# Query, key, value and four gate tiles of a hybrid layer: seven block products ahead of the attentions instead of plain products between them

## The chip, the cores and the metric

One core of a Trainium2 chip. The time is the device time of one execution in microseconds (us); of several runs the median is given. TensorE (PE) multiplies, ScalarE (ACT) and VectorE (DVE) work on SBUF and PSUM, GpSimd (POOL) does small work and issues some transfers, and SyncE (SP) issues most of them. PEld is TensorE's loading of weights, which overlaps its matmuls.

## The reference

One layer of an encoder for two requests that share all weights: a prompt of 1024 tokens and a sample of 32 tokens with a cache of 512. Model width 1024, 8 heads of 64 in either attention, feed-forward width 2816.

```python
ada = silu(c) @ w_ada + b_ada            # sh1, sc1, gt1, sh2, sc2, gt2
h = rms_norm(x, g_pre_mix) * (1 + sc1) + sh1
p = h @ w_in    # q-latent 384 | kv-latent 256 | rope key 32 | sb q 512 | sb k 512 | sb v 512 | gate A 1024 | gate B 1024
o_a = block-causal latent attention (softmax)
# o_b, stick-breaking attention, strictly causal:
z = q @ k.T * SB_SCALE
sp = where(mask, softplus(z), 0)
later = reverse_cumsum(sp) - sp
a = where(mask, exp(log_sigmoid(z) - later), 0);  o_b = a @ v
merged = sigmoid(g_a) * (o_a @ w_proj_a) + sigmoid(g_b) * (o_b @ w_proj_b)
x = x + gt1 * rms_norm(merged @ w_out, g_post_mix)
x = x + gt2 * rms_norm(conv_ffn(rms_norm(x, g_pre_ffn) * (1 + sc2) + sh2), g_post_ffn)
```

Outputs are both requests' rows, the latents, rope keys, keys and values of both, and the last rows of the convolution's state. All of it is float32.

## The kernel before

Both requests lie side by side as 1056 columns (1024 + 32): the activations are held transposed, 8 tiles of 128 features by 1056 tokens. Every float32 product is three matmuls: each operand is split into a high part (rounded by ACT, `hi`, L65) and a low part (the rest, subtracted by DVE, `lo`, L68), and `mm3` (L72 to L74) multiplies high by high, low by high and high by low into one PSUM bank.

`stage_h` is the opening. It loads the rows of x, scales them (`load`), computes the modulation of the norm in two halves (`ada_half(0)` and `ada_half(1)`: eight weight tiles from DRAM, four small matmuls each at L252, a copy, two transposes at L257, and the gain at L236), and turns the rows by TensorE (`norm_T`, L281); ACT applies gain and shift (`hf`), DVE casts the high part (L290) and takes the low one (L291). The result is `Hh` and `Hl`. The second half of the features needs the second gain.

`stage_sb` then runs four pairs of heads. Each `sb_pair` first makes its query, key and value tile of 128 columns of `w_in` with `mtile`: three blocks of 352 columns by 8 k by 3, 72 matmuls a tile. Queries and keys are split into parts, keys and values are turned into natural rows for the outputs (`to_natural`, L400) and stored on POOL's queue (L446). Then the pair's two heads go through attention block by block. The order of its work is written out by hand as a string of tokens, `ORDER`: S is a score (L473 and L474), a and e the two sigmoids on ACT, c a scan and x a product on DVE, T a transpose (L591), h and v its two parts, V the values (L605), o and p the output. Between them stand the filler tokens: f is one step of a generator `gates`, which computes a gate tile of `w_in` (72 matmuls, four tiles in each pair) and a few weight products of the modulation (`ada_step`), G takes its result out, D sums the modulation, W and w split the next weights. TensorE, ACT, DVE and POOL each keep that order. After each second pair `sb_sample` does the sample's attention (L747 and near it). A pair's first score follows its own value tile at once, so a new pair begins with 216 matmuls of products. `stage_lat` and the latent attention, the merge and the feed-forward follow; the feed-forward's up-projection already multiplies in halves with seven products instead of eight (L1683 to L1685).

Of the kernel before, what the change touches and what calls it, by code (L numbers as in the profile page):

```python
# [41 lines left out]
PARTS = ((0, 0, 96), (96, 80, 16), (112, 64, 16))  # L42


class K:
# [107 lines left out]
    def late_vectors(self):  # L153

        nc, a = self.nc, self.a
        v = self.tl(self.At, [P, TP], F32, "A")
# [83 lines left out]
    def ada_half(self, hf, wp, tp):  # L240
# [4 lines left out]
        for k in range(KT):  # L245

            last = hf == 1 and k >= KT - 2
            w = self.tl(*((self.W, [P, 1024]) if last else (wp, [P, 2 * 512])), F32, "wr").rearrange("p (v n) -> p v n", v=2)
# [17 lines left out]
    def norm_T(self, t0, xs, g, sv, tp, k0=0, k1=KT):  # L266


        nc = self.nc
        if t0 < 8:  # L270
            n = len(xs) * P
            m = 512 // n
            c = slice(t0 * P, t0 * P + n)
            for k in range(k0, k1, m):
                tr = self.bank("tr")
                f = self.tl(tp, [P, 512], F32, "hf").rearrange("p (k c) -> p k c", k=m)
                for e in range(m):
                    kc = slice((k + e) * P, (k + e) * P + P)
                    for j, x in enumerate(xs):
                        o = e * n + j * P  # L280
                        nc.tensor.transpose(tr[:, o : o + P], x[:, kc], self.idt)  # L281
                h, l = self.Hht[:, k : k + m, c], self.Hlt[:, k : k + m, c]

                both = t0 == 4 and k0 == 0
                for e in range(m):
                    for x in (f, h) if both else (f,):
                        nc.scalar.activation(x[:, e], tr[:, e * n : e * n + n], AF.Identity,
                                             bias=self.adaT[:, sv, k + e, 0:1], scale=g[:, k + e, 0:1])
                if not both:
                    nc.vector.tensor_copy(h, f)  # L290
                nc.vector.tensor_tensor(l, f, h.bitcast(F32), ALU.subtract)  # L291
        else:
            tr = self.bank("tr")
            for c in range(2):
                nc.tensor.transpose(tr[:, c * P : c * P + P], xs[0][:, c * P : c * P + P], self.idt)
            f = self.tl(tp, [P, 512], F32, "hf")[:, :256].rearrange("p (k t) -> p k t", t=TS)
            for k in range(k0, k1):
                j, c = k // 2, k % 2
# [104 lines left out]
    def sb_pair(self, p):  # L403
# [33 lines left out]
        def ev_out(name, after=None):  # L437
            def ev(tr, t0, n, r):
# [8 lines left out]
                if after:  # L447
                    after(st, tr, t0, n, r)
# [1781 lines left out]
```

## Time and profile before

| what | us |
| --- | --- |
| median of 3 runs | 1736.81 (1736.24 to 1738.41) |
| the profiled execution | 1738.68 |
| its span | 1736.8 |
| PE busy | 1697.2 |
| DVE busy | 1206.2 |
| ACT busy | 909.9 |
| POOL busy | 279.3 |
| first score of pairs 0, 1, 2, 3 at | 84.83, 201.30, 323.74, 438.99 |
| last value product of pairs 0, 1, 3 at | 163.91, 279.17, 516.87 |

The span runs from the first to the last instruction; what lies around it in an execution is 1.9 us here. In rows of the timeline the first number is the start, the second the time to the end of the last of the xN instructions, and the bracket tells the engine's idle time before and what ended it. In rows of groups, busy time and the mean of one in ns follow the bar, then the idle time before.

### The profile page before, as it was taken

How to read it: one execution, taken by the hardware profiler on the slowest of the kernel's cores; microseconds unless marked ns; L12 is line 12 of the kernel's file. 1: busy time of each engine (PE TensorE's matmuls, PEld its weight loads, DVE VectorE, ACT ScalarE, POOL GpSimd, SP SyncE). 2: the span in 40 equal slices, each digit the busy share in tenths (PEclk: the TensorE clock that was granted, in tenths of full speed). 3: DMA queues.
4: the chain of work that ended last, by engine and by line, in shares of the span. 5: the costliest groups of instructions: out<-in, count | busy, mean ns of one | idle time of the engine just before them, and what ended most of it. 6: DMA issues, size and time to landing. Idle time of an engine off the chain costs nothing. (4 is left out here: it accounts for less than half of the span.)

```text
span 1736.8 us, 29763 instructions
## 1 busy us (share of the span) xinstructions
PE 1697.2 (98%) x11542; PEld 1548.3 (89%) x11542; DVE 1206.2 (69%) x1971; ACT 909.9 (52%) x1745; POOL 279.3 (16%) x586
## 2 busy tenths in 40 slices
PE   6999999999999999999999999999999999999998
PEld 3899999999999988989888779999999999977886
DVE  4576574574662587768785778877787787788456
ACT  5455453553552677767774277444454444544442
POOL 2211111211120011101100032221111121110013
PEclk8999999999999999999999999999999999999999
DMA  8243333333341222222245631434323323697753
GB/s 321 82 133 103 108 107 97 99 120 92 112 120 49 74 74 64 64 72 66 100 163 179 190 128 43 164 104 128 128 92 128 128 92 128 210 343 241 238 148 119
DMA packets 170094, 223.64 MB, mean 129 GB/s; under 512 B 12917, under 2 KB 117056, under 8 KB 169952
## 3 DMA queue, kind: packets, MB, share of 16 engines
q1 hardware_dynamic: 154336, 177.91, 32.3%
q0 software_dynamic: 15392, 43.74, 7.1%
q8 instruction: 91, 1.49, 0.4%
q14 instruction: 51, 0.42, 0.1%
q10 hardware_dynamic: 224, 0.09, 0.0%
HBM read 169.92 MB, written 51.25 MB: 127 GB/s over the span
## 5 line engine op out<-in xcount | busy, mean ns | idle before, releaser
L65 ACT ACTIVATE wh<-wr 128x1024 fp32r<-128x1024 f32 (+6 forms) x161 | 134.4, 846 | 261.6 <-PE s L1684 80.0
L68 DVE TENSOR_TENSOR wl<-wr,wh 128x1024 fp32r<-128x1024 f32 (+6 forms) x161 | 153.0, 959 | 140.9 <-ACT wh L65 140.5
L72 PE MATMUL mm<-hh,wh 128*128 128x352 f32 x696 | 234.7, 337 | 0.0
L73 PE MATMUL mm<-hl,wh 128*128 128x352 f32 x696 | 226.9, 326 | 0.3 <-DVE hl L291 0.2
L74 PE MATMUL mm<-hh,wl 128*128 128x352 f32 x696 | 227.2, 326 | 0.0
L72 PEld LDWEIGHTS mm<-hh,wh 128*128 128x128 f32 x696 | 131.8, 189 | 9.0 <-issue 5.4
L73 PEld LDWEIGHTS mm<-hl,wh 128*128 128x128 f32 x696 | 131.7, 189 | 3.9 <-DVE hl L291 1.7
L74 PEld LDWEIGHTS mm<-hh,wl 128*128 128x128 f32 x696 | 131.4, 189 | 1.7 <-issue 1.6
L68 DVE TENSOR_TENSOR PTl<-tr,PTh 128x512 fp32r<-128x512 f32 x100 | 68.3, 687 | 50.6 <-ACT PTh L65 50.2
L1685 PE MATMUL s<-T,wl 128*128 128x256 f32 (+1 forms) x328 | 93.6, 285 | 0.0
L1683 PE MATMUL s<-T,wh 128*128 128x256 f32 (+1 forms) x328 | 93.3, 284 | 0.0
L1684 PE MATMUL s<-T,wh 128*128 128x256 f32 (+1 forms) x328 | 93.2, 284 | 0.0
L1824 DVE SCALAR_TENSOR_TENSOR u<-u,c,u 128x1058 f32<-128x1058 f32 x68 | 87.1, 1318 | 2.0 <-ACT u L1821 0.7
L65 ACT ACTIVATE PTh<-tr 128x512 fp32r<-128x512 f32 x100 | 59.3, 597 | 53.8 <-PE tr L591 51.0
L591 PE MATMUL tr<-c,A 128*128 128x128 f32 x576 | 83.5, 274 | 0.6 <-DVE A L693 0.5
L1683 PE MATMUL tr<-T,wh 128*128 128x272 f32 (+1 forms) x272 | 77.9, 286 | 0.0
L1685 PE MATMUL tr<-T,wl 128*128 128x272 f32 (+1 forms) x272 | 77.6, 285 | 0.0
L1684 PE MATMUL tr<-T,wh 128*128 128x272 f32 (+1 forms) x272 | 77.5, 285 | 0.0
L68 DVE TENSOR_TENSOR wl<-S,wh 128x1024 fp32r<-128x1024 f32 x40 | 49.0, 1224 | 37.4 <-ACT wh L65 36.1
L591 PEld LDWEIGHTS tr<-c,A 128*128 128x128 f32 x576 | 68.1, 140 | 5.9 <-issue 1.6
L1685 PE MATMUL mm<-T,wl 128*128 128x256 f32 (+1 forms) x256 | 73.0, 286 | 0.3 <-DVE wl L68 0.2
L1683 PE MATMUL mm<-T,wh 128*128 128x256 f32 (+1 forms) x256 | 73.1, 286 | 0.0
(682 smaller groups left out, 5385.1 us busy)
## 6 DMA issues: line engine op xcount, KB each, us to landing
wr<-in_w_ada_dram SPq DMA_DIRECT2D x48, 512.0 KB, 4.6
wr<-in_w_up_dram SPq DMA_DIRECT2D x44, 512.0 KB, 4.2
dr<-in_w_down_dram SPq DMA_DIRECT2D x43, 512.0 KB, 6.0
wr<-in_w_in_dram SPq DMA_DIRECT2D x33, 512.0 KB, 4.4
wr<-gdn SPq DMA_DIRECT2D x30, 512.0 KB, 4.7
gdn<-u POOLq DMA_DIRECT2D x23, 512.0 KB, 5.0
gd<-nat POOLq DMA_DIRECT2D x48, 176.0 KB, 2.3
t<-gd SPq DMA_DIRECT2D x16, 528.0 KB, 5.1
```

The lines of the kernel that those rows point to most:

```text
L65: self.nc.scalar.activation(out, in_, AF.Identity, scale=scale)
L68: return self.nc.vector.tensor_tensor(out, full, hi.bitcast(F32), ALU.subtract)
L72: m(ps, lh, rh, start=start, stop=False)
L73: m(ps, lh, rl, start=False, stop=False)
L74: self.pe = m(ps, ll, rh, start=False, stop=stop).ins
L591: self.nc.tensor.transpose(tr[:, (2 * s + q) * P : (2 * s + q + 1) * P], at[q][:, b * P : b * P + P], self.idt)
L1683: m(ps[:, :n], w[0][:, k], x[0][:, k, c], start=first and k == 0, stop=False, skip_group_check=True)
L1684: m(ps[:, :n], w[0][:, k], x[1][:, k, c], start=False, stop=False, skip_group_check=True)
L1685: i = m(ps[:, :n], w[1][:, k], x[0][:, k, c], start=False, stop=k == 3, skip_group_check=True)
L1824: nc.vector.scalar_tensor_tensor(y, u[:, w : w + YW], self.cvT[:, w, cc : cc + 1], y, ALU.mult, ALU.add)
```

## The change

A tile pair's product is cut into halves: the pair's two tiles of 128 columns of `w_in` (A), the two halves of the 1024 features, and the two halves of the 1056 columns (HC = 528, as 256 and 272). Winograd's form needs seven products of half size: with B11 and B22 and so on the quarters of h, they go over B11, T1, B21, T2, T3, T4 and B22, where T1 = B12 - B11, T3 = B22 - B12, T2 = T3 + B11 and T4 = B21 - T2. The sums of h are made once, on DVE, with their high parts on ACT; the sums of weights are made for each pair of tiles. `z_prod` is one product of 24 matmuls, `z_out` takes it out (a copy on ACT, or an addition on DVE), and the steps a to g are the seven products of a group.

There are eight groups: two of gates (tiles 0 and 1, 2 and 3), and (q0,k0), (v0,v1), (q1,k1), (q2,k2), (v2,v3), (q3,k3). Steps a and b of the first two stand inside `stage_h`, ahead of `ada_half(1)`. A new `stage_in` does all the rest ahead of the attentions. `z_done` splits queries, keys and values and writes them to scratch in DRAM; `sb_load` brings them back for each pair on POOL's queue, for pair 0 right behind the last stores. The quarter B12 of h is parked in DRAM and split again by the filler token B inside pair 0. Twelve gate tiles are left as filler, three in a pair, in four blocks of 264 columns, as are the latents; the weight products of the modulation go 3, 3 and 2 with the three tiles of a pair; and `ORDER` is written anew for this. Cut to its core:

```diff
+        self.F = [[self.u_tile().rearrange("p (k c) -> p k c", k=2) for _ in range(2)] for _ in range(2)]
...
             for t in range(4):
                 load(t)
             self.ada_half(0, wp, tp)
             norm(0, 0)
-            w = [self.w_in_tile(672)]
+            g0, g1 = self.early = self.group(0), self.group(1)
+            self.raw_a(g0)
             for t in range(4, 8):
                 load(t)
...
+            self.raw_b(g0)
             norm(4, 0)
...
+            self.step_a(g0, "mm mm")
+            for i in range(2):
+                x = self.F[1][i]
+                self.plus(x, self.F[0][i], B11, i, ALU.subtract)
+                self.both(T1, x, i)
+            self.raw_a(g1)
+            self.step_b(g0, "mm mm")
+            self.raw_b(g1)
+            self.step_a(g1, "mm mm")
+            self.step_b(g1, "mm mm")
             self.ada_half(1, wp, tp)
-            nc.vector.tensor_scalar(xs, xs, self.rstd_s(xs, tp), None, ALU.mult)
             norm(0, 1)
-            norm(8, 0)
             norm(4, 1)
             norm(8, 1)
...
+    def plus(self, out, x, pair, i, op):
+        for b in pair:
+            self.nc.vector.tensor_tensor(out, x, b.bitcast(F32)[:, 2 * i : 2 * i + 2], op)
+            x = out
+    def both(self, d, x, i):
+        h, l = (y[:, 2 * i : 2 * i + 2] for y in d)
+        self.hi(h, x)
+        self.lo(l, x, h)
...
+    def unit(self, x):
+        if self.n_unit % 2 == 0:
+            self.wt = [self.tl(self.W, [P, 1024], F32R, t) for t in ("wh", "wl")]
+        i = 512 * (self.n_unit % 2)
+        self.n_unit += 1
+        h, l = (t[:, i : i + 512] for t in self.wt)
+        self.hi(h, x)
+        self.lo(l, x, h)
+        return [t.rearrange("p (k c) -> p k c", k=4) for t in (h, l)]
+    Z_BLK = ((0, 256), (256, 272))
+    def z_prod(self, w, x, tags=None, banks=None):
+        new = banks is None
+        if new:
+            banks = [self.bank(t) for t in tags.split()]
+        for (c0, n), ps in zip(self.Z_BLK, banks):
+            c = slice(c0, c0 + n)
+            for k in range(4):
+                for i, (p, q) in enumerate(((0, 0), (0, 1), (1, 0))):
+                    self.nc.tensor.matmul(ps[:, :n], w[p][:, k], x[q][:, k, c], start=new and k + i == 0,
+                                          stop=k == 3 and i == 2, skip_group_check=True)
+        return banks
+    def z_out(self, out, banks, x=None):
+        for (c0, n), ps in zip(self.Z_BLK, banks):
+            c = slice(c0, c0 + n)
+            if x is None:
+                self.nc.scalar.copy(out[:, c], ps[:, :n])
+            else:
+                self.nc.vector.tensor_tensor(out[:, c], ps[:, :n], x[:, c], ALU.add)
+    def step_a(self, g, tags):
+        w = self.unit(g["ra"][:, :512])
+        g["q1"] = self.tl(self.Zq, [P, HC], F32, "q1", 3)
+        self.z_out(g["q1"], self.z_prod(w, self.Z["B11"], tags))
+    def step_b(self, g, tags):
+        add = self.nc.vector.tensor_tensor
+        s = g["s1"] = self.tl(self.Zq, [P, 512], F32, "s1", 2)
+        add(s, g["rb"][:, :512], g["rb"][:, 512:], ALU.add)
+        w = self.unit(s)
+        q = g["q5"] = self.tl(self.Zq, [P, HC], F32, "q5", 2)
+        self.z_out(q, self.z_prod(w, self.Z["T1"], tags))
+        self.nc.gpsimd.tensor_tensor(q, q, g["q1"], ALU.add)
...
+    def step_d(self, g, tags):
+        ra, rb, add = g["ra"], g["rb"], self.nc.vector.tensor_tensor
+        add(rb[:, :512], ra[:, :512], rb[:, :512], ALU.subtract)
+        add(ra[:, :512], g["s1"], ra[:, :512], ALU.subtract)
+        X = g["X"] = self.z_prod(self.unit(ra[:, :512]), self.Z["T2"], tags)
+        g["q2"] = self.tl(self.Zp, [P, HC], F32, "q2", 2)
+        self.z_out(g["q2"], X, g["q5"])
+    def step_e(self, g):
+        self.z_prod(self.unit(g["rb"][:, :512]), self.Z["T3"], None, g["X"])
+        g["ub"] = self.u_tile()
+        self.z_out(g["ub"][:, HC:], g["X"], g["q5"])
+    def step_f(self, g):
+        self.z_prod(self.unit(g["rb"][:, 512:]), self.Z["T4"], None, g["X"])
+        self.z_out(g["ub"][:, :HC], g["X"], g["q1"])
+        self.z_done(g["cols"][1], g["ub"])
+    def step_g(self, g, tags):
+        ra = g["ra"]
+        self.nc.vector.tensor_tensor(ra[:, 512:], ra[:, 512:], ra[:, :512], ALU.subtract)
+        w = self.unit(ra[:, 512:])
+        self.z_out(g["ua"][:, HC:], self.z_prod(w, self.Z["B22"], tags), g["q2"])
+        self.z_done(g["cols"][0], g["ua"])
...
+        self.step_c(g0, "s s")
+        for i in range(2):
+            nc.vector.tensor_tensor(F1[i], F2[i], F1[i], ALU.subtract)
+        for i in range(2):
+            self.plus(F2[i], F1[i], Z["B11"], i, ALU.add)
+            self.both(Z["T2"], F2[i], i)
+        self.step_c(g1, "s pv")
+        for i in range(2):
+            self.both(Z["T3"], F1[i], i)
+        self.step_d(g0, "mm mm")
+        for i in range(2):
+            b = [x.bitcast(F32)[:, 2 * i : 2 * i + 2] for x in Z["B21"]]
+            nc.vector.tensor_tensor(F2[i], b[0], F2[i], ALU.subtract)
+            nc.vector.tensor_tensor(F2[i], F2[i], b[1], ALU.add)
+            self.both(Z["T4"], F2[i], i)
+        self.step_d(g1, "tr tr")
+        self.out_c(g0)
+        self.step_e(g0)
+        self.step_f(g0)
+        self.step_g(g0, "s s")
+        self.out_c(g1)
+        self.step_e(g1)
+        self.step_f(g1)
+        self.step_g(g1, "s pv")
+        for n in range(2, len(self.PAIRS)):
+            g = self.group(n)
+            self.raw_a(g)
+            self.raw_b(g)
+            self.step_a(g, "s s")
+            self.step_b(g, "s pv")
+            self.step_c(g, "s s")
+            self.out_c(g)
+            self.step_d(g, "mm mm")
+            self.step_e(g)
+            self.step_f(g)
+            self.step_g(g, "s pv")
+            if n == 2:
+                self.late_vectors()
...
+        if i == 0:
+            h = hs()
+            self.hi(r(h), u[:, :TP], 0.125)
+            nc.scalar.mul(self.qsb[:, p], u[:, TP:], 0.125)
+            nc.vector.scalar_tensor_tensor(ur, u[:, :TP], 0.125, h, ALU.mult, ALU.subtract)
+            nc.gpsimd.dma_start(self.qhd[p], h)
+            nc.gpsimd.dma_start(self.qld[p], u[:, :TP])
+            return
...
+        if i == 1:
+            nc.gpsimd.tensor_copy(self.ksb[:, p], u[:, TP:])
+            h = hs()
+            self.hi(r(h), u[:, :TP])
+            self.lo(ur, u[:, :TP], r(h))
+            nc.gpsimd.dma_start(self.khd[p], h)
+            nc.gpsimd.dma_start(self.kld[p], u[:, :TP])
...
+    def sb_load(self, p):
+        dma = self.nc.gpsimd.dma_start
+        lo, hi = slice(0, 64), slice(64, 128)
+        qh, ql, kh, kl = self.qhd[p], self.qld[p], self.khd[p], self.kld[p]
+        ops = []
+        for r, KL in zip((lo, hi), self.KLz):
+            o = hi if r is lo else lo
+            Q, KH = (self.tl(self.Sp, [P, TP], F32R, n, b) for n, b in (("Q", 3), ("KH", 2)))
+            dma(Q[r], qh[r])
+            dma(Q[o], ql[r])
+            dma(KH[lo], kh[r])
+            dma(KH[hi], kh[r])
+            dma(KL[r], kl[r])
+            ops.append((Q, KH, KL))
+        V = self.tl(self.Sp, [P, 8, 2, P], F32R, "V", 1)
+        dma(V, self.vd[p])
+        return ops, V
+    def sb_pair(self, p):
         nc = self.nc
...
+        ops, V = self.sb_load(p)
...
-        S1.0 f2 a1.0 f e1.0 f S0.0 c1.0 f a0.0 f e0.0 f x1.0 f c0.0 x0.0 S0.1 f D a0.1 S1.1 e0.1 c0.1 f a1.1
+        S0.1 a0.1 f e0.1 c0.1 f x0.1 S0.0 S1.0 a0.0 e0.0 c0.0 a1.0 x0.0 e1.0 S2.0a c1.0 S2.0b a2.0a T0.0
+        a2.0b x1.0 h0.0 c2.0a S1.1 e2.0a v0.0 a1.1 c2.0b f e1.1 f e2.0b c1.1 f B W f2 x1.1 f B f w f2 B V0.0
...
+            for i, m in enumerate(ms):
+                yield from self.ada_step((3, 3, 2)[i % 3], self.W, self.At, ada)
...
+            elif kind == "B":
+                if back:
+                    k = back.pop(0)
+                    x, (h, l) = self.f12[k // 2][:, k % 2], (y[:, k] for y in self.B12)
+                    self.hi(h, x)
+                    self.lo(l, x, h)
...
+        self.fill = self.gates(range(4, 16))
```

TensorE at the end of the opening. Names: `hh`, `hl` are the parts of h, H_22 and H_23 those of T1, `s_98` or `s_125` the sum of the modulation, `wr` its weights, `ada1` its copy. Before:

```order
L252 MATMUL s_98_351<-wr_103_376,cT_119 32x256 x4
L73 MATMUL mm_142_584<-hl_16_94,wh_63_258 128x352
L74 MATMUL mm_142_584<-hh_15_93,wl_64_259 128x352
L252 MATMUL s_98_351<-wr_104_382,cT_119 32x256 x4
L252 MATMUL s_98_351<-wr_105_388,cT_119 32x256 x4
L252 MATMUL s_98_351<-wr_106_394,cT_119 32x256 x4
L257 MATMUL s_107_401<-c_1_70,ada1_97_350 128x128 x2
L72 MATMUL s_147_646<-hh_15_93,wh_86_304 128x352
L73 MATMUL s_147_646<-hl_16_94,wh_86_304 128x352
L74 MATMUL s_147_646<-hh_15_93,wl_87_305 128x352
```

After:

```order
L458 MATMUL mm_123_499<-H_22_111,wl_116_461 128x272
L458 MATMUL mm_123_499<-H_22_111,wh_115_460 128x272
L458 MATMUL mm_123_499<-H_23_112,wh_115_460 128x272
L458 MATMUL mm_123_499<-H_22_111,wl_116_461 128x272
L259 MATMUL s_125_528<-wr_131_559,cT_146 32x256 x3
L259 MATMUL s_125_528<-wr_132_565,cT_146 32x256 x4
L259 MATMUL s_125_528<-wr_133_571,cT_146 32x256 x4
L264 MATMUL s_134_578<-c_1_70,ada1_124_527 128x128 x2
L283 MATMUL tr_139_602<-c_1_70,b12l_21_100 128x128 x2
L283 MATMUL tr_139_602<-c_1_70,b12h_20_99 128x128 x2
L458 MATMUL s_157_708<-H_16_95,wh_155_704 128x256
```

The last weight products of the second gain and their transposes (L264) stood behind the first products of 352 columns; now they stand behind 48 products with T1 (and 48 with B11), and what follows, B21's products (H_16), needs the second gain.

DVE behind the second gain. Names: `u_26` and `u_27` hold the quarters and then the sums, H_150 and H_152 are the low parts of T3 and T2, `b12l` that of T4, `q2` and `u_169` results of products, `wl_171` the low weights of step e. Before, these were first of the pair's own work:

```order
L416 SCALAR_TENSOR_TENSOR Q_139_553<-mm_142_584,Q_139_553 64x352
L417 SCALAR_TENSOR_TENSOR Q_140_554<-mm_142_584,Q_140_554 64x352
L731 MEMSET QZ_541_3052 128x256
L68 TENSOR_TENSOR wl_160_757<-wr_158_754,wh_159_756 128x1024
L416 SCALAR_TENSOR_TENSOR Q_139_553<-mm_143_613,Q_139_553 64x320
L417 SCALAR_TENSOR_TENSOR Q_140_554<-mm_143_613,Q_140_554 64x320
L68 TENSOR_TENSOR wl_172_867<-wr_170_864,wh_171_866 128x1024
```

After:

```order
L531 TENSOR_TENSOR u_24_118<-u_26_120,u_24_118 128x1056
L531 TENSOR_TENSOR u_25_119<-u_27_121,u_25_119 128x1056
L408 TENSOR_TENSOR u_26_120<-u_24_118,H_14_93 128x1056
L408 TENSOR_TENSOR u_27_121<-u_25_119,H_14_93 128x1056
L408 TENSOR_TENSOR u_26_120<-u_26_120,H_15_94 128x1056
...
L77 TENSOR_TENSOR H_150_676<-u_24_118,H_149_675 128x1056
L77 TENSOR_TENSOR H_152_678<-u_26_120,H_151_677 128x1056
...
L541 TENSOR_TENSOR u_26_120<-H_16_95,u_26_120 128x1056
L469 TENSOR_TENSOR q2_165_808<-mm_164_783,q5_111_428 128x272
L542 TENSOR_TENSOR u_26_120<-u_26_120,H_17_96 128x1056
...
L77 TENSOR_TENSOR b12l_154_680<-u_26_120,b12h_153_679 128x1056
...
L77 TENSOR_TENSOR wl_171_856<-wr_90_321,wh_170_855 128x512 x2
```

Queries' low parts, weights and keys stood there; now it is the sums and low parts of four quarters of h, with additions of finished products between them, and the low weights of T3's first product come behind all of them.

TensorE between products and the first attention. Names: `mm_163` is the value tile of pair 0 and `pv_397` the last product of the last group, `s_` are scores, KLz and KH keys, `wr` weights of the modulation. Before:

```order
L72 MATMUL mm_163_812<-hh_15_93,wh_159_756 128x352
L73 MATMUL mm_163_812<-hl_16_94,wh_159_756 128x352
L74 MATMUL mm_163_812<-hh_15_93,wl_160_757 128x352
L400 MATMUL tr_164_838<-c_1_70,big_157_753 128x128 x4
L400 MATMUL tr_166_848<-c_1_70,big_157_753 128x128 x4
L473 MATMUL s_177_896<-KH_144_643,Q_139_553 128x384
L474 MATMUL s_177_896<-KLz_137_549,Q_139_553 128x384
L400 MATMUL tr_168_858<-c_1_70,big_157_753 32x128
L203 MATMUL mm_178_899<-wr_180_905,cT_119 32x256
```

After:

```order
L458 MATMUL pv_397_2651<-H_18_97,wh_387_2590 128x272
L458 MATMUL pv_397_2651<-H_19_98,wh_387_2590 128x272
L458 MATMUL pv_397_2651<-H_18_97,wl_388_2591 128x272
L669 MATMUL s_418_2757<-KH_412_2736,Q_411_2735 128x256
L670 MATMUL s_418_2757<-KLz_402_2719,Q_411_2735 128x256
L212 MATMUL mm_419_2761<-wr_421_2767,cT_146 32x256 x4
L212 MATMUL mm_419_2761<-wr_422_2775,cT_146 32x256 x4
L669 MATMUL s_425_2785<-KH_412_2736,Q_411_2735 128x256
```

The transposes of values that stood between the last product and the first score are done earlier, and the first scores have no product behind them but eight small ones of the modulation.

POOL at the same place, after the change; `qhd3`, `qld3`, `khd3` and `kld3` are the scratch of the last group (pair 3), `kld0` that of pair 0's low keys:

```order
L618 DMA khd3_695<-hs_395_2642 128x1024
L619 DMA kld3_699<-u_386_2587 128x1024
L587 DMA qhd3_687<-hs_398_2678 128x1024
L588 DMA qld3_691<-u_380_2523 128x1024
L656 DMA KLz_402_2719<-kld0_696 64x1024
L652 DMA Q_413_2742<-qhd0_684 64x1024
L653 DMA Q_413_2742<-qld0_688 64x1024
```

The load of pair 0's low keys stands behind the stores of the last group on this queue; before, there was no such load, since keys stayed in SBUF.

More of the change, by code (lines that the diff above doesn't have):

```diff
@@ L275, in norm_T @@
                 tr = self.bank("tr")
[L276 to L291, printed above, removed]
+                for j, x in enumerate(xs):
+                    nc.tensor.transpose(tr[:, j * P : j * P + P], x[:, q * P : q * P + P], self.idt)
```

310 lines of the change are left out of this document (173 added, 137 removed).

## The prediction

> **What bounds the kernel now.** I read the page's busy times and slices first, then the chain of waits of TensorE up to 560 us (where everything the change touches lies), then windows, then the timeline around the places that move.
>
> ```profile
> PE 1697.2 (98%) x11542; PEld 1548.3 (89%) x11542; DVE 1206.2 (69%) x1971; ACT 909.9 (52%) x1745; POOL 279.3 (16%) x586
> PE   6999999999999999999999999999999999999998
> ...
> PE tr L706 <- DVE A L619: 1.3, 2, 0.6
> PE s L756 <- ACT A L748: 0.3, 2, 0.2
> ```
>
> TensorE is busy 98% of the span, slices 2 to 39 are full, and between 47.4 and 560 us it waited 1.6 us in all. So every TensorE microsecond taken out of this stretch is worth one, as long as nothing else becomes late; equally every new wait costs its full length.
>
> ```profile
> 170.00:185.00 15.00, 15.00 (x95) 15.00 (x94) 3.79 (x8) 3.94 (x8) 0.00 (x0) 1.00 0.12 36
> 1186.49:1247.94 61.45, 61.45 (x507) 61.45 (x504) 48.34 (x73) 29.12 (x47) 13.68 (x31) 1.00 0.41 132
> 201.30:279.20 77.90, 77.90 (x558) 73.34 (x557) 57.84 (x89) 42.81 (x94) 14.18 (x38) 1.00 0.42 129
> 1060.00:1160.00 100.00, 99.33 (x818) 97.33 (x818) 90.98 (x125) 52.35 (x87) 23.57 (x44) 1.00 0.33 111
> 40.00:46.00 6.00, 6.00 (x65) 3.44 (x57) 1.20 (x3) 0.98 (x3) 0.81 (x4) 0.89 0.00 1
> 1014.00:1016.00 2.00, 2.00 (x6) 1.55 (x5) 0.00 (x0) 1.51 (x3) 0.62 (x2) 0.53 0.00 0
> 1016.00:1018.00 2.00, 2.00 (x8) 1.54 (x7) 0.59 (x2) 1.25 (x3) 0.00 (x0) 0.62 0.03 8
> ```
>
> Columns: busy time and count of PE, PEld, DVE, ACT, POOL, then clock, DMA share, GB/s. Row one is nothing but 352-column products of the old kind: some 93 starts in 15.00 us, 161 ns each. Row two is the feed-forward stage, which already multiplies by seven products with 256- and 272-column pieces: 504 matmuls in 61.45 us, 122 ns each. Row three is one whole attention (pair 1): TensorE full, DVE 57.84 of 77.90 us. Row four: with DVE at 91%, TensorE still idles only 0.7 us in 100.
>
> ```profile
> 44.83 1.50 PE L252 MATMUL s<-wr,cT 128*32 128x256 f32 x24
> 47.62 0.17 DVE L236 SCALAR_TENSOR_TENSOR c<-c,c 128x8 f32<-128x8 f32 x1
> 84.83 0.42 PE L473 MATMUL s<-KH,Q 128*128 128x384 f32 x1
> 163.91 0.28 PE L605 MATMUL pv<-PTl,V 128*128 128x256 f32 x1
> 200.29 1.25 PE L400 MATMUL tr<-c,big 128*128 128x128 f32 x8
> 201.30 0.42 PE L473 MATMUL s<-KH,Q 128*128 128x384 f32 x1
> 279.17 0.28 PE L605 MATMUL pv<-PTl,V 128*128 128x256 f32 x1
> 323.74 0.42 PE L473 MATMUL s<-KH,Q 128*128 128x384 f32 x1
> 516.87 0.28 PE L605 MATMUL pv<-PTl,V 128*128 128x256 f32 x1
> 1012.82 0.55 PE L1637 MATMUL tr<-c,t 128*128 128x128 f32 x3 [1.86 <-ACT t L65]
> ```
>
> These are my landmarks: the second gain of the norm at 47.6, the first score of pair 0 at 84.8, the end of each attention (L605) and the last one's at 516.9. Query, key and value tiles of pair 1 fill 163.9 to 201.3 (37.4); 279.2 to 323.7 is 44.6, the 7.2 more being the sample's attention. The L400 row gives 0.14 us for a transpose, (1.25-0.27)/7.
>
> **The products.** Sixteen tiles of 72 matmuls were 1152 x 0.161 = 185.5 us; eight groups of 7 x 24 are 1344 x 0.122 = 164.0. That removes 21.5 us. The other gate tiles and the latents go from 72 x 0.161 = 11.59 to 96 x 0.122 = 11.71 (264 columns, nearest to the 256/272 row): 18 tiles, +2.2. A rule to hold against this: the Trainium skill, "TensorE: Matmul & The Clock Gate", section "Wait — 56ns, not 53.3ns?", gives a warm matmul N/2.4 GHz plus about 2.5 ns, an estimate of 149 and 112 ns here. By it the 21.5 would be 20.7. The two rows of this kernel carry 10 to 12 ns more for each matmul, and they decide.
>
> The gain is thus known to about 1 us. Whether it arrives depends on four places, which I walk along TensorE's order.
>
> **1. The opening.** The last weight products of the second gain now stand behind the T1 products of two groups. T1 needs four 1056-column subtractions and two low parts on DVE, which had 4.8 us free in 40:46.
>
> ```profile
> L1534 DVE TENSOR_TENSOR t<-t,t 128x1056 f32<-128x1056 f32 x8 | 10.0, 1256 | 0.2
> L68 DVE TENSOR_TENSOR ml<-t,mh 128x1056 fp32r<-128x1056 f32 x8 | 10.1, 1258 | 0.9 <-ACT mh L65 0.7
> L291 DVE TENSOR_TENSOR hl<-hf,hh 128x512 fp32r<-128x512 f32 x16 | 10.9, 686 | 4.8 <-ACT hh L287 4.6
> L290 DVE CAST hh<-hf 128x512 fp32r<-128x512 f32 x8 | 3.4, 423 | 1.6 <-ACT hf L287 1.5
> L1760 DVE TENSOR_TENSOR u<-s,q 128x256 f32<-128x256 f32 x120 | 50.4, 420 | 8.5 <-PE s L1685 4.9 <-ACT q L1796 3.4
> L287 ACT ACTIVATE hf<-tr,c,c 128x512 f32<-128x512 f32 x16 | 12.1, 776 | 12.4 <-DVE c L236 6.9 <-PE tr L281 4.0 <-DVE hh L290 0.9
> ```
>
> From about 41: 4 x 1.256 + 2 x 1.258 = 7.5, so T1 at 48.5 (bounds 45 and 55, since its rows stand behind the norms of ACT and DVE, which may be later). Then 70 matmuls (8.5), the 11 remaining weight products (11/24 x 1.5 = 0.7) and, as between 46.3 and 47.8 now, 1.5 for copy, transposes and gain: second gain at 59.2 instead of 47.8. TensorE has done 96 products by then instead of 24 old ones, so the loss is only 3 us or so.
>
> **2. The sums of the half matrices.** Everything behind the second gain goes through DVE in one row. After the first hf (0.78 us): four casts and four low parts of 512 columns, 4 x (0.42+0.69) = 4.4; the same of the other half, 4 x 0.41 + 4 x 0.67 = 4.3 (scaled to 496 columns), and 0.9 of small pieces; six 1056 sums 7.5; four low parts 5.0; then four more sums 5.0, two low parts 2.5, and between them six additions of 256/272 columns 2.6; and two halves of weights (512 columns, as L291), 1.4. Sum 33.7. Only then does TensorE get the low weights wl of T3's first product. Until that row it has 108 matmuls and 16 transposes, 13.2 + 2.2 = 15.4 us. So it stands at 59.2 + 0.8 + 33.7 = 93.7 and has then 132 matmuls, 16.1 us, of the two groups left: 109.8. Without the wait they would end at 59.2 + 31.5 = 90.7: a wait of 19 us, in two or three pieces. Bounds: 0, if T2 to T4 were ready when wanted, and 23, if ACT's high parts are late too.
>
> After a wait comes the clock. A pause of 1.86 us ahead of 1012.82 is followed by 0.53 and 0.62 of the clock in the two windows above: 2 x 0.47 + 2 x 0.38 = 1.7 us lost. I charge it once here: 111.5.
>
> **3. Six groups and the way through scratch.** The rows for what stands on DVE, POOL and its queue:
>
> ```profile
> L1824 DVE SCALAR_TENSOR_TENSOR u<-u,c,u 128x1058 f32<-128x1058 f32 x68 | 87.1, 1318 | 2.0 <-ACT u L1821 0.7
> L446 POOL DMA_DIRECT2D out_dram<-nat x24 | 16.9, 710 | 41.9 <-ACT nat L440 31.3 <-issue 10.6
> L2116 POOL TENSOR_TENSOR u<-d,u 128x512 f32<-128x512 f32 x7 | 11.7, 1683 | 134.9 <-DVE d L2097 90.7 <-DVE d L2076 36.0 <-DMA out_dram<-u 8.1
> ...
> out_dram<-nat POOLq DMA_DIRECT2D x20, 256.0 KB, 4.6
> ```
>
> 42 products of 24, 123.0; 72 transposes, 10.1, as before; late vectors and one small wait, 1.7: 246.3. What a group asks of DVE is some 14 us in 20.5 (seven low parts of weights and four sums of 512 columns at 0.69, fourteen additions at 0.42), and POOL's one addition per group 1.7 (row L2116): both stay covered. The loads of a following pair, eleven with 3.5 MB, have a whole attention of 66 us, where the DMA share was 0.42.
>
> The low keys of pair 0 (KLz) are loaded on POOL's queue behind the last store of the last query tile. Price from the last product on: addition 0.42, low part 1.3, two issues 1.4, landing 4.6 (256 KB, the nearest row): 7.8, and 1.7 of clock, 9.5. Only eight small weight products stand there as cover. Bounds: 5 (a landing half as long, no clock) and 13 (two landings in turn). First score at 255.8.
>
> **4. The attentions.** Each loses its old filler (four gate tiles, 288 matmuls, 46.4) for 288 of 264 columns, 35.1: 77.9 - 46.4 + 35.1 = 66.6, four times 266.4. DVE's work stays at 57.84, now 87% of it. By the row of 1060:1160 that costs TensorE 0.7%, 2 us in all. The sample's 7.2 now stands between two attentions without products beside it: 3 more. Bounds for both: 0 and 20 (a DVE that cannot work ahead). End of the last attention: 255.8 + 266.4 + 7.2 + 5 = 534.4, against 516.9: +17.5, and with the latents' share of the narrower blocks (6 tiles, 0.7) +18.2. Behind that nothing moves. The profiled execution of before took 1738.7 (its span 1736.8 and 1.9 around it), 1.9 above the median of the runs: 1756.9, as a median **1755**.
>
> **Rivals.**
>
> *The sums are hidden after all.* Then place 2 costs 1.8 where I charge 19 + 1.7, and the time is 1755 - 19 - 1 = 1735: not slower. For it: DVE has slack everywhere else, and TensorE could be kept busy if the sums came in time. Against it: the 1.256 rows are of exactly this kind of operand, and DVE takes its rows in order. It decides from a chain under 17 us instead of 33.7.
>
> *The attentions become DVE's.* With 87% in the mean, but scans and low parts in bursts, a pair could take 71 instead of 66.6: 4 x 4.4 - 2 = +16, 1771. For it: the same DVE work in 11 us less. Against it: the 91% row.
>
> *The opening is cheap and the transition is hidden.* T1 at 45 and a first score 5 us after the last product: 3.5 + 4.5 less, 1747; still slower. This is the lower part of my own case.
>
> **How the numbers follow.** The forecast, 1745 to 1766, has 0.60; the hidden sums 0.22, of which 0.13 lie under 1733.3 (0.2% below 1736.8, about what a measurement of this kernel can tell from no change) and 0.09 between that and 1740.3; DVE-bound attentions 0.18, all slower. So faster 0.13, same 0.09, slower 0.78. The range reaches from 1733 to 1771: it leaves out about 0.12 below and 0.08 above.
>
> **What would show it.** Right: TensorE idle by some 19 us between 60 and 95, ended by DVE's sums and low parts, with the clock near half behind; a wait of 6 to 10 us ahead of the first score, ended by a load of KLz; 122 ns for each product; the last attention's end near 534. Wrong: the two groups' end near 91, or attention stretches well over 67 us each with TensorE waiting for DVE.

## The result and the profile after

The changed kernel takes 1803.62 us, median of four runs (1803.12 to 1807.12), against 1737.61 before: a ratio of 1.0385 (95% interval 1.0367 to 1.0403). It is 66 us slower, where +18 was forecast and 1771 was the upper end of the range. The profiled execution has a span of 1802.2 us.

The page, in the lines that answer to those of before (busy time and share of each engine; TensorE's and its clock's share in 40 slices):

```profile
PE 1700.7 (94%) x12168; PEld 1542.5 (86%) x12168; DVE 1282.9 (71%) x2125; ACT 922.3 (51%) x1797; POOL 331.0 (18%) x668
PE   4799977999999999999999999999999999999997
...
PEclk7899987999999999999999999999999999999999
```

TensorE is no longer full: beside the opening (slices 1 and 2) now slices 6 and 7 (225 to 315 us) have holes, and its clock drops with them. TensorE's idle time grew from 39.6 to 101.5 us. Its busy time is no smaller than before (1700.7 against 1697.2), although the products alone took away about 19: behind the waits the same work takes longer, as at 288 us, where at half the clock two 264-column products start 220 ns apart. The waits of TensorE, longest sums first (engine, line, what it waited for: us in all, times, the longest):

```profile
PE mm L212 <- DMA wr<-in_w_ada_dram: 17.5, 3, 13.4
PE s L670 <- DMA KLz<-kld: 10.5, 1, 10.5
PE tr L159 <- DMA gb<-in_b_ada_dram: 8.5, 1, 8.5
PE s L259 <- DMA wr<-in_w_ada_dram: 8.2, 5, 2.8
```

Two single waits, 10.5 and 13.4 us, stand out. The windows of the stretches that the prediction spoke of (columns as there):

```profile
40.00:50.00 10.00, 9.25 (x42) 5.67 (x42) 7.12 (x12) 5.70 (x14) 1.91 (x4) 0.51 0.41 110
50.00:60.00 10.00, 7.20 (x54) 5.01 (x51) 3.93 (x5) 1.51 (x2) 0.00 (x0) 0.83 0.69 250
80.00:90.00 10.00, 7.01 (x43) 6.58 (x42) 10.00 (x9) 5.27 (x6) 0.00 (x0) 0.83 0.01 2
90.00:100.00 10.00, 6.49 (x49) 5.84 (x48) 10.00 (x13) 3.21 (x4) 0.00 (x0) 1.00 0.00 0
141.20:255.70 114.50, 113.56 (x910) 110.35 (x909) 71.98 (x128) 41.40 (x83) 40.75 (x66) 1.00 0.55 171
255.70:286.20 30.50, 5.93 (x32) 3.77 (x31) 10.43 (x20) 6.58 (x16) 8.53 (x21) 0.59 1.10 295
506.04:572.78 66.74, 64.79 (x537) 59.62 (x536) 53.75 (x88) 40.08 (x95) 13.82 (x38) 1.00 0.45 134
```

In the opening the clock is low (0.51, then 0.83). Between 80 and 100 us DVE is busy all the time and TensorE two thirds. From 141 to 255.7, five whole groups, TensorE is full. Then come 30.5 us in which it works 5.9 at 0.59 of the clock while the DMA engines run at a share of 1.10 (295 GB/s). The last row is pair 3's attention, 66.74 us long. The timeline at that hole, TensorE, and the transfers that POOL's and SyncE's queues issue in it (start, us of issuing):

```profile
256.35 0.38 PE L669 MATMUL s<-KH,Q 128*128 128x256 f32 x1 [0.62 <-DMA KH<-khd]
267.28 0.58 PE L670 MATMUL s<-KLz,Q 128*128 128x256 f32 x1 [10.55 <-DMA KLz<-kld]
286.24 0.65 PE L212 MATMUL mm<-wr,cT 128*32 128x256 f32 x4 [13.44 <-DMA wr<-in_w_ada_dram]
...
258.85 0.53 POOL L588 DMA_DIRECT2D qld<-u  x1 [0.41 <-DVE o L1016]
259.51 0.52 POOL L656 DMA_DIRECT2D KLz<-kld  x1
264.14 0.58 POOL L659 DMA_DIRECT2D V<-vd  x1 [0.75 <-DMA qhd<-hs]
...
266.13 0.33 SPq L1025 DMA_DIRECT2D qt<-in_k_ropeq_dram  x1
266.51 0.89 SPq L1045 DMA_DIRECT2D big<-f12d  x2
268.07 1.74 SPq L208 DMA_DIRECT2D ada<-in_b_ada_dram  x4
269.92 0.36 SPq L210 DMA_DIRECT2D wr<-in_w_ada_dram  x1
```

The second score waits for the low keys, which are issued behind the last store. The next small products at L212 wait for a third weight tile of the modulation, which SyncE issues at 269.92, behind the rope table, the two halves of the parked quarter and the biases. That queue had issued nothing between 254 and 266.1, when the store of the last queries (qld) landed.

Place by place, forecast against measured (us):

| place | forecast | measured |
| --- | --- | --- |
| second gain | 59.2 | 70.3 |
| end of the two opening groups | 111.5 | 119.1 |
| last product | 246.3 | 255.7 |
| second score (low keys there) | 255.8 | 267.3 |
| third weight of the modulation | no wait | 286.2 |
| end of the last attention | 534.4 | 572.8 |
| span | 1755.0 (1736.8 + 18.2) | 1802.2 |

### The profile page after: what moved, and what is told of

Read it like the earlier page. It is cut to its first block, busy times and chain, and to the rows that moved or that the text cites. A ratio compares the mean times of both kernels' runs of the same rounds, so it can differ in the third digit from the quotient of the medians.

```text
span 1802.2 us, 31433 instructions
## 1 busy us (share of the span) xinstructions
PE 1700.7 (94%) x12168; PEld 1542.5 (86%) x12168; DVE 1282.9 (71%) x2125; ACT 922.3 (51%) x1797; POOL 331.0 (18%) x668
## 5 line engine op out<-in xcount | busy, mean ns | idle before, releaser
L74 ACT ACTIVATE wh<-wr 128x1024 fp32r<-128x1024 f32 (+5 forms) x169 | 132.3, 798 | 292.5 <-PE s L1881 78.9
L77 DVE TENSOR_TENSOR wl<-wr,wh 128x1024 fp32r<-128x1024 f32 (+5 forms) x169 | 152.6, 913 | 108.3 <-ACT wh L74 106.8
L81 PE MATMUL mm<-H,wh 128*128 128x264 f32 x360 | 107.9, 300 | 0.0
L82 PE MATMUL mm<-H,wh 128*128 128x264 f32 x360 | 103.9, 289 | 0.0
L83 PE MATMUL mm<-H,wl 128*128 128x264 f32 x360 | 103.6, 288 | 0.0
L77 DVE TENSOR_TENSOR wl<-S,wh 128x1024 fp32r<-128x1024 f32 (+1 forms) x64 | 66.8, 1047 | 38.2 <-ACT wh L74 37.9
L74 ACT ACTIVATE wh<-S 128x1024 fp32r<-128x1024 f32 (+1 forms) x64 | 57.0, 896 | 55.1 <-PE s L1881 13.2
L2011 POOL COPY c<-u 128x2 f32<-128x2 f32 x44 | 26.5, 603 | 259.6 <-DVE u L1957 224.5
L81 PEld LDWEIGHTS mm<-H,wh 128*128 128x128 f32 x360 | 69.4, 193 | 5.2 <-issue 4.5
L1881 PE MATMUL mm<-T,wh 128*128 128x272 f32 (+1 forms) x256 | 72.8, 285 | 0.0
```

What stands on the lines that cost most here:

```text
L74: self.nc.scalar.activation(out, in_, AF.Identity, scale=scale)
L77: return self.nc.vector.tensor_tensor(out, full, hi.bitcast(F32), ALU.subtract)
L81: m(ps, lh, rh, start=start, stop=False)
L82: m(ps, lh, rl, start=False, stop=False)
L83: self.pe = m(ps, ll, rh, start=False, stop=stop).ins
L1881: m(ps[:, :n], w[0][:, k], x[1][:, k, c], start=False, stop=False, skip_group_check=True)
```

## Experiments

All are the changed kernel with an edit. Each gave four runs (the last one five); the median, its ratio to the kernel before with the interval, and the span of the profiled execution are:

| run | median us | ratio | span |
| --- | --- | --- | --- |
| changed kernel | 1803.62 | 1.0385 (1.0367 to 1.0403) | 1802.2 |
| sums_left_out | 1776.74 | 1.0224 (1.0209 to 1.0240) | 1774.6 |
| values_last | 1802.92 | 1.0367 (1.0348 to 1.0387) | 1802.7 |
| weights_first | 1797.34 | 1.0349 (1.0331 to 1.0366) | 1795.5 |
| second_gain_first | 1796.94 | 1.0341 (1.0317 to 1.0365) | 1794.1 |
| gates_last | 1796.58 | 1.0333 (1.0311 to 1.0355) | 1792.9 |
| three_together | 1790.58 | 1.0305 (1.0266 to 1.0345) | 1784.6 |
| stores_by_sync | 1802.30 | 1.0360 (1.0327 to 1.0393) | 1793.8 |
| three_and_no_sums | 1768.98 | 1.0179 (1.0152 to 1.0207) | 1765.9 |
| more_bytes | 1805.55 | 1.0393 (1.0350 to 1.0436) | 1811.8 |
| space_early | 1793.73 | 1.0330 (1.0315 to 1.0345) | 1793.0 |
| weights_early | 1793.33 | 1.0338 (1.0307 to 1.0370) | 1789.1 |
| five_together | 1783.30 | 1.0261 (1.0247 to 1.0275) | 1785.3 |

Runs of one kernel lie up to 11 us from their median (more_bytes: 1794.4 to 1813.6), so differences of a few us are read from the place in the trace, not from the totals. A place scatters too, by less: over the runs in which the opening and the sums are not edited, the two opening groups end between 117.5 and 120.9 us, and over those in which the transition (last product to third weight) is not edited, it lasts 30.0 to 31.6.

**DVE's row of sums.** In `stage_in`:

```diff
-        Z["T3"], Z["T2"] = self.two(T23), self.two(T23)
-        Z["T4"] = self.two(self.Hp, "b12")
+        Z["T2"], Z["T3"], Z["T4"] = Z["B22"], Z["B22"], Z["B21"]
...
-            (the sums F1, F2 and both() for T2, T3, T4)
```

> This kernel leaves out the sums T2, T3 and T4 of the half matrices (their products take other quarters of h instead, so the same matmuls run on other data); everything else is as in the changed kernel, whose span was 1802.2 us. Theory: DVE's row of sums and low parts behind the second gain (69.7 us there) holds TensorE until about 101 us. Without it the two opening groups should end near 104 instead of 119.1, and the span be 14 to 18 us shorter, 1784 to 1788. Rival: TensorE is held in that stretch by the norm's own parts and the clock, and the sums cost little: the end of the two groups moves by under 5 us and the span stays above 1797.

The two groups ended at 104.9 instead of 119.1, 14.2 us earlier, as the theory had it; 0.9 of it is scatter, since the second gain, ahead of which nothing was edited, came at 69.4 instead of 70.3. The waits of TensorE between 70 us and there:

```profile
PE tr L283 <- ACT hf L284: 1.8, 1, 1.8
```

With the sums, the same stretch has these beside it:

```profile
PE mm L458 <- ACT H L74: 2.1, 1, 2.1
...
PE s L458 <- DVE H L298: 1.9, 1, 1.9
PE tr L458 <- ACT wh L74: 1.6, 1, 1.6
PE tr L458 <- DVE q L469: 1.3, 1, 1.3
PE s L458 <- DVE u L469: 1.0, 1, 1.0
```

But the span fell by 27.6 where 14 to 18 were expected: the wait for the low keys was gone too. T2 and T3 fill the SBUF space into which pair 0 is loaded; without them the loads went before the last stores. The run space_early, below, tests that alone.

**The order of the groups, and of SyncE's queue.** Three edits at the transition:

```diff
-    ... (672, 2, 1184, 2), (1696, 2, 1696, 3), (672, 3, 1184, 3)     # values_last
+    ... (672, 2, 1184, 2), (672, 3, 1184, 3), (1696, 2, 1696, 3)
```

> The order of the groups is changed so that the value group (v2,v3) is the last and (q3,k3) the one before. Theory: pair 0's low keys and SyncE's queue wait for the last group's stores of queries (2 MB, and the SBUF space that they read). With values last, 1.5 MB are stored there and none of them waits for a low part: the wait ahead of the second score falls from 10.5 to about 7 us, the one for the modulation's weights from 13.4 to about 10, the span to about 1795. Rival: the stretch from 255.7 to 286.2 us is set by the bytes that all queues have to move in it (9 MB at 295 GB/s): the first wait may be shorter, the second grows by as much, and the span stays within 3 us of 1802.

The first wait rose to 14.1, the second fell to 6.5, and the work went on at 285.8 instead of 286.2. That is the rival's span, though it had the first wait shrink and the second grow. I had miscounted what the group stores, two value tiles with outputs and scratch, 3.1 MB and not 1.5.

```diff
-        nc.sync.dma_start(self.qt, self.a["k_ropeq"])                # weights_first: moved to p == 2
...
+                if count[0] == 3:                                    # behind the third weight
+                    for i in range(2): nc.sync.dma_start(self.f12[i], self.f12d[i])
```

> On SyncE's queue the loads of the rope table (0.5 MB) go behind pair 1, and the second of the two loads of the parked quarter goes behind the third weight tile of the modulation, which then stands third from the front; the four tokens that split the parked quarter stand some 10 filler steps later. Theory: the 13.4 us wait for that weight comes from its place behind 1.6 MB on the same queue; it should fall to 4 to 6 us and the span to 1792 to 1795. Rival one: bytes decide, and only the 0.5 MB moved away count, 2 us: 1800. Rival two: the queue stands still until the last store of queries has landed (266 us), and the wait ends at 272 at the earliest, whatever the order: 1790 to 1793.

The wait for the weight fell from 13.4 to 9.5, that for the low keys rose from 10.5 to 11.5; the work went on 27.2 us behind the last product instead of 30.5. Those 3.3 us lie between the two theories, nearer to bytes: 1.1 MB (9.00 to 7.88, in the table below) left the stretch, since the parked quarter now comes behind the weight as well, and at 295 GB/s that is 3.8 us.

```diff
+    PAIRS = [(x, x + P) for x in (2208, 672, 1184, 1696, 928, 1440, 1952, 2464)]   # gates_last
```

> The groups are (gate 0, gate 1), (q0,q1), (k0,k1), (v0,v1), (q2,q3), (k2,k3), (v2,v3) and, last, (gate 2, gate 3): the last group stores 1.1 MB of gates instead of 2.6 MB of keys and queries, and pair 0's scratch is complete long before. Theory: the bytes that must pass between the last product and the third weight of the modulation set that stretch (9 MB at 295 GB/s in 30.5 us); 1.5 MB less is 5 us: span 1796 to 1798. Rival: what counts is that the low keys stand behind the last product's store on POOL's queue and that SyncE's queue stands still until that store has landed; both stay, and the span stays within 2 us of 1802.

The hole shrank from 30.5 to 25.7, the 5 us of the theory.

**Bytes or order?** Two copies within DRAM are added, and nothing else:

```diff
+        if p == 0:
+            for n in "ab":
+                dma(self.dr.tile([P, TP], F32, name="copy" + n), self.khd[3])
         dma(V, self.vd[p])
```

> Two extra copies of 0.5 MB within DRAM (khd3 to places that nothing reads) are issued on POOL's queue between the second load of low keys and that of the values, at about 263 us; nothing else is changed. Theory: between the last product and the third weight of the modulation the queues move bytes at 295 GB/s and nothing else sets the time; 1.05 MB more makes the wait for that weight 3.5 us longer (up to 7, if a copy counts as a read and a write), and the span likewise. Rival: the place on SyncE's queue sets it (still until 266 us, then four transfers one after the other); the copies are on another queue, and the wait grows by under 1 us.

The hole grew from 30.5 to 32.6 us, more than the rival allowed (1) and less than the theory asked (3.5). Beside the 31.6 of an unedited transition only 1.0 of it is clear of scatter; the wait for the third weight itself is clearer, 15.3 against 12.6 to 13.5. The traffic in the hole, from the last product to the third weight: the changed kernel, then three_together, then more_bytes.

```profile
DMA packets 3411, 9.00 MB, mean 295 GB/s; under 512 B 409, under 2 KB 1516, under 8 KB 3281
```

```profile
DMA packets 1717, 6.06 MB, mean 294 GB/s; under 512 B 285, under 2 KB 413, under 8 KB 1587
```

```profile
DMA packets 3548, 10.09 MB, mean 309 GB/s; under 512 B 444, under 2 KB 1629, under 8 KB 3386
```

| run | MB in the hole | us | GB/s |
| --- | --- | --- | --- |
| three_together | 6.06 | 20.6 | 294 |
| gates_last | 7.49 | 25.7 | 292 |
| weights_first | 7.88 | 27.2 | 290 |
| changed kernel | 9.00 | 30.5 | 295 |
| values_last | 9.23 | 30.2 | 306 |
| more_bytes | 10.09 | 32.6 | 309 |

Whatever is moved, the mean rate stays at 290 to 309 GB/s with a share of 1.09 and more, and the added copies appear in full (9.00 to 10.09 MB). So in this stretch the DMA engines are the bound, and a queue's order counts by the bytes that it puts ahead of the transfer waited for. A constant rate alone would make bytes and time proportional in any case; what shows the cause are the edits that change the bytes: 1.5 MB less shortened the hole by 4.8 us (gates_last) and 2.9 MB less by 9.9 (three_together), far outside the scatter. These two change the order as well; more_bytes changes bytes alone and points the same way, by little. The Trainium skill ("DMA: Bandwidth & Descriptors", section "Issuing engines are not separate DMA queues") says that transfers of all issuing engines run on the same 16 DMA engines and interleave; these six stretches agree: POOL's and SyncE's queues (5.78 and 3.20 MB of the 9.00 in the changed kernel) together keep to the 290 to 309 GB/s.

That rate belongs to this mix and is no constant of the engines. In the opening of the kernel before, a share of 1.05 went with 399 GB/s:

```profile
16.00:20.00 4.00, 3.52 (x43) 1.38 (x42) 0.00 (x0) 0.00 (x0) 0.00 (x0) 1.00 1.05 399
```

**The space of T2 and T3.**

```diff
-    ... self.Z["T2"] ... / self.Z["T3"] ...
+    ... self.Z["B22" if g["n"] == 7 else "T2"] ... / "T3" likewise
```

> Only the last group takes B22 in place of T2 and T3 (its two results are not the reference's), all sums are made as before. So the SBUF space of T2 and T3, into which pair 0's keys and queries are loaded, comes free one group (22.7 us) earlier. Theory: that space is why the loads crowd behind the last product; now seven or eight of the eleven go ahead of the last stores, the 10.5 us wait for the low keys vanishes and the span falls by 10 to 14 us, as it did for the transition's part when the sums were left out altogether. Rival: bytes alone count, 2 MB moved ahead of the last product are 6 to 7 us. Rival two: DVE's row, not the space, was the whole gain there: under 3 us.

The wait for the low keys vanished and the span fell by 9.2 us (the median by 9.9), between the theory and the bytes alone. The rest came back at once. The waits of TensorE and of DVE there:

```profile
PE tr L778 <- DVE A L731: 13.7, 3, 9.2
DVE ptd L1021 <- DMA qld<-u: 8.5, 1, 8.5
```

DVE now waits for the last store of queries, whose space the attention's own tiles take, and TensorE for DVE. So 9 of the 13 us by which sums_left_out won more than at the sums are the space.

**The opening.**

```diff
+            self.ada_half(1, wp, tp)          # ahead of raw_a(g1) ... step_b(g1); norms behind step_a(g1)
```

> In the opening the second half of the modulation and the norms of the second half of the features stand ahead of T1's products and of the second group's first products. Theory: the second gain comes at 53 to 56 us instead of 69.7, T1's 48 products stand beside DVE's row of sums, and the two groups end 10 to 14 us earlier (105 to 109 instead of 119.1); span 1788 to 1792. Rival: the modulation's weights have four buffers and their loads set the second gain, at 60 or later; and DVE's row, longer by T1's weights, takes the rest: the two groups end at 114 or later and the span stays above 1797.

The second gain came at 55.2, the two groups ended at 112.1 (7.0 earlier), between the theory (105 to 109) and the rival (114), and TensorE still waited 3.3 us for the weights of the modulation.

```diff
-            w = self.tl(wp, [P, D], F32, "wr", 4)
+            w = self.tl(wp, [P, D], F32, "wr", 5)   # and the stores of f12d behind ada_half(1)
```

> As the second gain first in the opening (which had it at 55.2 us), and besides one more buffer for the modulation's weights (5 for 4), and the parked quarter (1.1 MB) is stored behind those weights' products. Theory: with TensorE's products out of the way, the second gain waits for the loads of these weights, which wait for a free buffer: it comes at 51 to 53. Rival: the loads are bound by what the queue moves ahead of them (rows of x and the weights of two groups), and it stays at 55. In both cases the span is within 4 us of 1794.

The gain came at 53.0, as the theory had it, and the wait was gone: the weights had waited for a buffer, for the parked quarter's stores, or for both, which this run does not separate. The groups ended at 110.4.

**The drain at the end.**

```diff
-                nc.gpsimd.dma_start(self.gd[m, :, c0 : c0 + n], g[:, :n])
+                nc.sync.dma_start(self.gd[m, :, c0 : c0 + n], g[:, :n])
```

> The 48 stores of the filler's gate tiles (one after each block of 264 columns) are issued on SyncE's queue instead of POOL's. At the end of the program POOL drains for 10.3 us, against 4.8 in the kernel before, which issues 251 transfers on POOL's queue instead of 325. Theory: the drain grows with the transfers that POOL has issued, 75 ns for each: with 277 left it takes 6.7 us and the span falls by 3 to 4 us. Rival one: it goes by the bytes or packets, of which these stores are 6.5 of 72 MB: 9.8 us. Rival two: it has to do with the loads from scratch and stays at 10.3. SyncE's own loads may be held up behind a store that waits for its data: the attention stretches may grow by up to 3 us each.

The program's last line, POOL's sequencer, before, after and in this run (shortest, median, longest of three drains in ns):

```profile
L2226 POOLq DRAIN  x3: 46/93/4762, 1731.3 to 1736.6; - x3
```

```profile
L2424 POOLq DRAIN  x3: 46/98/10317, 1791.1 to 1801.9; - x3
```

```profile
L2424 POOLq DRAIN  x3: 46/98/5907, 1787.1 to 1793.5; - x3
```

Taking 48 transfers off POOL's queue shortened the drain by 4.41 us, where the theory had 3.6 and the rivals had 0.5 and nothing. That would be 92 ns for each transfer, but a price for each is not shown: more_bytes issues two more on this queue (327) and drains for 10.316 us, the same to 1 ns, and from the 277 here to the 251 of the kernel before it is 1.14 us, 44 ns each. The total did not show it (1802.30, with runs from 1795.6 to 1806.4; the profiled one is 8.4 us shorter, of which 4.4 are the drain).

**Together.** The edits of weights_first, second_gain_first and gates_last in one kernel, then without the sums, then with weights_early and stores_by_sync added:

> The three edits together: the second gain first in the opening, the third weight ahead on SyncE's queue, the gates as last group. If they act at different places, their gains add: 7 to 8 (two opening groups end at 112 instead of 119), 5 to 7 and about 5, a span of 1782 to 1785. If the transition is bytes alone, the second and third give 7 together: 1787 to 1789. In no case is it below the kernel before (1736.8): what is left is the wait of DVE's row, some 15 us of transition, and the way through scratch.

> As the three edits together, and besides the sums T2, T3 and T4 are left out (other quarters of h stand in for them), which also frees the SBUF space of T2 and T3. It tells how far the rest is from the kernel before. If DVE's sums and the space that T2 and T3 hold are all that is left, the span falls to about 1755: 1784 less 14 for the two groups and 15 for the transition. If the bytes through scratch bound the transition whatever the space, it is 1765 to 1770.

> All edits that computed the reference and helped, in one kernel: the second gain first with five weight buffers and the late store of the parked quarter, the third weight ahead on SyncE's queue, the gates as last group, and the filler's stores on SyncE's queue. If each keeps what it gave alone beside the three together (span 1784.6), 2 for the earlier gain and 4.4 for the drain come off: 1777 to 1780. If SyncE's queue is held up by the stores, the third weight's wait or the attentions grow and it stays at 1783 or more. It does not come below the kernel before (1736.8) in either case.

Place by place the three add: the groups end 5.7 us earlier (113.4) and the hole is 9.9 shorter, together 15.6, where each alone had 7.0, 3.3 and 4.8. The total does not decide between the two cases: the profiled span is 1784.6, but the four runs' spans reach from there to 1798.8, with a median of 1788.8. Without the sums 1765.9, at the edge of the second case: the transition still has waits of 5.4 and 1.6 us. The five together take 1783.3, a median span of 1781.5 (1785.3 in the profiled run), between the 1777 to 1780 and the 1783 or more of the two cases: the second gain came at 52.0, but TensorE waited 13.0 us in all for weights of the modulation (10.7 with three edits). It is the best of the versions that leave nothing out, and 2.6% slower than the kernel before; none beat that one.

## Why the prediction was wrong

The direction held, the size did not: +65.4 in the span against +18.2. The miss of 47.2 us by place: opening and sums 7.6, six groups 1.8, second score 2.1, from there to the end of the last attention 26.9, behind it 3.2, the drain 5.5.

- *The products* were right: a group runs as forecast (six groups 136.6 us against 134.8), and within a stretch of T1's and B11's products (61.27 to 66.64 us) the 45th matmul starts 5.37 us behind the first, 44 steps of 122 ns, the 122 of the rows. By the Trainium skill ("TensorE: Matmul & The Clock Gate", section "Wait — 56ns, not 53.3ns?") they would take an estimated 112; the 122 ns of the trace do not bear that out here.
- *Place 1* failed in two inputs. I priced 70 matmuls at the full clock, and up to 60 us they ran at 0.51 and 0.83 of it; and I took the weights of the modulation as there, though the change gives them four buffers instead of eight. The gain came 11 us late. second_gain_first and weights_early show the part of the weights; the clock is read from the windows and was not tried by itself.
- *Place 2* was right in its mechanism: DVE's row ran from 71.1 to 101.9, 30.8 us against 33.7. Its size was off: counted from the second gain, the sums cost the two groups 13.4 with the clock behind them (48.8 against the 35.5 of sums_left_out), where I charged 20.7. But without any wait I had 31.5 instead of 35.5, and the gain was 11.1 late; the three partly cancelled to about the 7.6, which is luck.
- *Place 3* is the step that failed, by 15.5 of the 47.2 (2.1 and 13.4). "Price from the last product on: ... landing 4.6" took the landing of a transfer from a quiet stretch. Here nine MB pass in 30.5 us; KLz, issued at 259.51, is there at 267.2, 7.7 us later. And I looked at POOL's queue alone. SyncE's queue, which the new order also brings to this place (space, rope table, parked quarter, biases, weight), gave the longest wait of the kernel, 13.4 us, and had no term in the sum at all; the "eight small weight products" that I called cover were followed by one that waited. The bound of 13 was one of a load, not of a queue of loads.
- *Place 4*: pair 3 takes 66.74 against 66.6 forecast, but that is not like for like: only 270 of a pair's 288 filler products lie between its first score and its last value product, and the other 18, 2.2 us, follow. So pair 3 costs some 2.3 us more than forecast, and 1.9 of it is a wait for a weight of the modulation. Pair 0 takes 71.4 without the long wait and pair 1 69.5, both without those 2.2. The attentions are still not DVE's: behind the hole TensorE's waits on DVE come to 4.3 us in all (rows below), where that rival had 16. Of the 26.9 us, 13.4 are the third weight. The other 13.5 come on top of the 5 that I allowed. In these 18.5 the trace lists 9.7 us of waits: 4.1 for two more weights of the modulation, 4.3 on DVE and 1.3 on ACT. The rest, part of which is a low clock (0.68 from 433 to 440 us), no run here takes apart.
- *Behind* the attentions 3.9 us were added where I had 0.7; this stays open, as latents and merge were not tried by themselves. "Behind that nothing moves" also put the drain at nothing: it took 10.32 us instead of 4.76. stores_by_sync took 4.4 of these 5.5 us back by issuing 48 stores elsewhere; what the drain goes by is open.
- The rival "sums are hidden" is refuted twice: they cost 13 to 14 us, and without them the kernel is still 2.2% slower.

The waits of TensorE on DVE in the attentions, behind the hole:

```profile
PE pv L792 <- DVE o L766: 2.7, 2, 1.9
PE tr L893 <- DVE A L806: 1.6, 1, 1.6
```

## What to carry to other kernels

A way through scratch is priced by the bytes that all queues must move between the last producer and the first consumer, at the rate that a trace shows for such a mix with full DMA engines (here some 295 GB/s), not by the landing of one transfer; and the loads can go early only if their SBUF space is free early, so look at what lies in it. When a block of work is moved, write down what every queue holds at the new seam, the quiet ones too: the wait here came from the queue that the change did not mention. Work that hides a chain of sums has to be there before the chain starts, and a product that gates such a chain goes ahead of products that do not.

## What was not expected of the hardware

POOL's drain at the end of the program depends on what this engine has issued, but not by one price for each transfer: it took 10.32 us with 325 and with 327 transfers, 5.91 with 277 (in two kernels), and 4.76 with the 251 of the kernel before, where it ends together with the last output. What it goes by is open. Second, the DMA engines kept a mean of 290 to 309 GB/s through six mixes of stores, loads and copies within DRAM, well under the 399 of the opening's loads at about the same share.
